# A fused two-block transformer layer: expert outputs with tokens stationary and 512 feature columns moving, and streamed activations and weight rooms on other sides of SBUF

## The chip, the core and the metric

The kernel runs as one program on one core of a Trainium2 chip. Its engines are TensorE (PE, matmuls; PEld is its loading of stationary operands), VectorE (DVE), ScalarE (ACT), GpSimd (POOL) and SyncE (SP, which issues the DMAs here). SBUF is the working memory with 128 partitions, PSUM the accumulators that PE writes. The metric is device time in microseconds, the median of several runs.

## What is computed

The reference is two blocks, one after the other, on 256 tokens of 1024 features. What matters here is the end of the first block, a mixture of 128 x 128 = 16384 experts of which each token uses 128 (8 heads, 16 each):

```python
    expert = (i1 * N_KEYS + i2).reshape(TOKEN_BLOCK, PEER_HEADS * PEER_TOPK)
    gate = jax.nn.softmax(best_s, axis=-1).reshape(TOKEN_BLOCK, PEER_HEADS * PEER_TOPK).astype(hx.dtype)
    u_sel = u[expert]
    v_sel = v[expert]
    act = jax.nn.gelu(jnp.einsum('nd,ned->ne', hx, u_sel), approximate=False)
    return jnp.einsum('ne,ned->nd', gate * act, v_sel)
```

Its result is scaled by `gate2` and added to x. The second block then projects `rms_norm_2(x) @ w_in`, runs a recurrence and a sparse attention, mixes them through `w_out`, and ends with a feed-forward part (`w_up`, a short convolution, a gelu, `w_down`).

## The kernel before

Instead of gathering experts, the kernel computes all 16384 activations for all tokens (the u loop, `u_unit`), multiplies them by a dense matrix of gates that is zero for experts not chosen (`gate_batch`), and multiplies the product by all of v (the v loop, L841 to L872).

**Weights.** All large weights come as units of 512 KB, [128, 8, 128] in fp32, in one fixed order (`stream`, L106): w1, wup1, wout1, wpq, u (128 units), v (128), w2, wup2, wout2, wff (48), wdn (24). SP loads a unit into `raw`, ACT writes its rounded part wh (L164), and DVE, or POOL for part of u, the rest wl (L165). A product is thus three matmuls: wh with the activation's high part, wh with its low part, wl with its high part (`mm3`, L188). All are of type float32r.

**Rooms.** wh and wl of a unit lie in a room, which holds a fixed number of units; a unit is split when its room has a place, up to four units ahead (`weights`, `prefetch`, L146 to L178). The plan (L139) says which room by position: w (two units, for all stages), a (stage one), b ("wwbb": two units of four, from unit 8 of w1 to the end of wout1), q, c ("wwcc", from the third unit of u to its 61st), d (three units, `spare`, v from unit 64), e ("wwe", from w2 to the end).

**Sides.** Pools are stacked from two ends of SBUF. Pools with no side or `side="left"` grow from the left: constants, raw, w, then what a stage opens. Pools with `side="right"` grow from the right end. Before the change, on the left: w, the room a, h2 (L644), the scratch of top-k, the gates' tiles (`pab`), the products `prh` and `prl` (pool pp, in h2's place), then hb, oh and hf (b2h, b2o) and xc. On the right: the first h, the room b below it, mix of the first block far down that stack, the activations actA and actB, room c below them, `spare` (the place of actA's first 24 rows), room e at the very end, and below it the attention's tiles and later ff (L1385).

**The u loop.** 128 units of 24 matmuls: stationary are 128 x 128 of weights, moving are 256 tokens of h2. Top-k of the scores runs beside the first half on DVE, one step per unit; gate batches for actA beside the second half.

**The v loop.** Per unit i, which holds 128 experts by 1024 features: for two units at a time ACT copies the gated activations into prh and DVE writes prl (L847, L848). Then 24 matmuls, for each of 8 feature blocks d three parts: stationary is u.h or u.l of block d, moving is pr with 256 tokens; the result lies in four banks vo, features on partitions. For i < 64 some 32 gate batches for actB are interleaved. Each has two products by gates (a2), two steps for b8, one for eqa on DVE, 16 small matmuls gt on PE, and a product into actB on DVE (L803); the last belongs to i = 57. From i = 64 on, every eighth unit computes one column of ada (8 of them) with the broadcast vector c (`cb`), which is loaded ahead of the loop.

**The end of v** (L875 to L900). For each of 8 feature chunks m: DVE forms x (L888, from vo, ada and x), ACT and DVE write hb's high and low part (L266, L267), and PE multiplies chunk m with the first three units of w2 (first3). A bank vo is complete once its last d is done, so the first chunks of x start while v still runs. The order of DVE's steps around it is fixed by manual dependencies (`chunk order`).

**Order.** The program's order is set by the loops; a scheduler places instructions of each engine by their dependencies and waits for tiles are set tile by tile.

## Time and profile before

| | |
|---|---|
| median of 3 runs | 1613.43 us |
| lowest, highest | 1612.01, 1619.1 us |
| profiled execution, its own time | 1618.32 us |
| its span | 1616.6 us |
| mean granted clock | 0.986 |
| PE, PEld, DVE, ACT, POOL busy | 97%, 93%, 78%, 51%, 13% of the span |
| HBM read | 277.92 MB, 173 GB/s over the span |

The profile is one execution of the program. Busy times of engines are unions of their instructions' times; the ends of matmuls are modelled, so that for matmuls the distance from one start to the next is the better measure. "Idle before" is time in which an engine stood still ahead of an instruction, with the one that released it. The granted clock is the share of TensorE's full clock (2.4 GHz).

### The profile page before, as it was taken

What the parts mean: (1) busy time and instruction counts of PE and PEld (TensorE: products, weight loads), DVE (VectorE), ACT (ScalarE), POOL (GpSimd) and SP (SyncE); (2) the same over time, 40 slices, a digit from 0 to 9 for tenths busy, and PEclk for the clock granted to TensorE, in tenths of its full rate; (3) what the DMA queues carried; (4) which work ended last, traced back from release to release, by engine and by line L of the source; (5) the groups of instructions that cost most, each with busy time, mean ns of one, the idle gap of its engine ahead of it and who ended that gap; (6) DMA issues with size and microseconds to landing.
All of it is one profiled execution on the core that took longest, in us unless ns stands there. A gap on an engine that the chain in (4) does not pass through costs nothing. (4 is left out here: it accounts for less than half of the span.)

```text
span 1616.6 us, 32864 instructions
## 1 busy us (share of the span) xinstructions
PE 1565.8 (97%) x13326; PEld 1509.9 (93%) x13326; DVE 1267.8 (78%) x2405; ACT 827.3 (51%) x1434; POOL 210.7 (13%) x156
## 2 busy tenths in 40 slices
PE   4999998999999999999999999998999999999999
PEld 3989998999999999999999999988977889999999
DVE  8789899984788887999856566979666666799963
ACT  3455563445444445443444444656656564576642
POOL 0100136795000000000000000035000000111100
PEclk9899999999999999999999999989999999999999
DMA  8668443555545545544566667453422224555553
GB/s 316 230 219 302 167 148 133 208 174 190 162 165 169 166 165 180 171 159 168 170 208 210 212 209 225 153 170 105 145 91 79 92 88 152 179 183 185 186 200 121
DMA packets 77927, 281.09 MB, mean 174 GB/s; under 512 B 8648, under 2 KB 9936, under 8 KB 77776
## 3 DMA queue, kind: packets, MB, share of 16 engines
q1 hardware_dynamic: 77776, 279.00, 51.6%
q8 instruction: 104, 1.70, 0.4%
q14 instruction: 47, 0.39, 0.1%
HBM read 277.92 MB, written 1.05 MB: 173 GB/s over the span
## 5 line engine op out<-in xcount | busy, mean ns | idle before, releaser
L164 ACT ACTIVATE wh<-raw 128x1024 fp32r<-128x1024 f32 x409 | 432.5, 1059 | 474.6 <-PE mm L188 244.8
L165 DVE TENSOR_TENSOR wl<-raw,wh 128x1024 fp32r<-128x1024 f32 x359 | 450.8, 1257 | 109.4 <-ACT wh L164 108.9
L852 PE MATMUL vo<-prh,spare 128*128 128x256 f32 x1024 | 181.1, 281 | 0.0
L852 PEld LDWEIGHTS vo<-prh,spare 128*128 128x128 f32 x1024 | 158.1, 190 | 0.0
L188 PE MATMUL mm<-h2h,wl 128*128 128x256 f32 x1024 | 143.6, 283 | 5.5 <-DVE wl L165 5.5
L188 PE MATMUL mm<-h2h,wh 128*128 128x256 f32 x1024 | 147.0, 286 | 0.0
L852 PE MATMUL vo<-prh,wh 128*128 128x256 f32 x512 | 146.7, 288 | 0.2 <-ACT prh L847 0.2
L188 PE MATMUL mm<-h2l,wh 128*128 128x256 f32 x1024 | 144.8, 285 | 0.0
L852 PE MATMUL vo<-prl,wh 128*128 128x256 f32 x512 | 144.5, 283 | 0.1
L254 POOL TENSOR_TENSOR r<-r,sq 128x256 f32<-128x256 f32 x18 | 14.5, 804 | 996.6 <-ACT sq L253 996.6
L852 PE MATMUL vo<-prh,wl 128*128 128x256 f32 x512 | 144.3, 283 | 0.0
L852 PE MATMUL vo<-prl,spare 128*128 128x256 f32 x512 | 143.9, 281 | 0.0
L165 POOL TENSOR_TENSOR wl<-raw,wh 128x1024 fp32r<-128x1024 f32 x50 | 134.2, 2701 | 68.6 <-ACT wh L164 41.6
L188 PEld LDWEIGHTS mm<-h2h,wl 128*128 128x128 f32 x1024 | 132.1, 192 | 5.9 <-DVE wl L165 5.9
L188 PEld LDWEIGHTS mm<-h2l,wh 128*128 128x128 f32 x1024 | 133.1, 193 | 0.0
L188 PEld LDWEIGHTS mm<-h2h,wh 128*128 128x128 f32 x1024 | 131.8, 192 | 0.2
L165 DVE TENSOR_TENSOR spare<-raw,spare 128x1024 fp32r<-128x1024 f32 x64 | 78.4, 1225 | 62.8 <-ACT spare L164 62.7
L164 ACT ACTIVATE spare<-raw 128x1024 fp32r<-128x1024 f32 x64 | 67.8, 1059 | 92.2 <-PE vo L852 89.5
L852 PEld LDWEIGHTS vo<-prl,wh 128*128 128x128 f32 x512 | 98.0, 191 | 0.2 <-DVE prl L848 0.2
L852 PEld LDWEIGHTS vo<-prh,wh 128*128 128x128 f32 x512 | 97.8, 191 | 0.3 <-ACT prh L847 0.3
L852 PEld LDWEIGHTS vo<-prh,wl 128*128 128x128 f32 x512 | 97.8, 191 | 0.2 <-DVE wl L165 0.2
L852 PEld LDWEIGHTS vo<-prl,spare 128*128 128x128 f32 x512 | 96.1, 188 | 0.0
(412 smaller groups left out, 3262.2 us busy)
## 6 DMA issues: line engine op xcount, KB each, us to landing
raw<-in_u_dram SPq DMA_DIRECT2D x128, 512.0 KB, 3.5
raw<-in_v_dram SPq DMA_DIRECT2D x128, 512.0 KB, 3.7
raw<-in_w_dram SPq DMA_DIRECT2D x86, 512.0 KB, 4.0
raw<-in_wada_dram SPq DMA_DIRECT2D x48, 512.0 KB, 5.0
raw<-in_wff_dram SPq DMA_DIRECT2D x48, 512.0 KB, 4.2
raw<-in_wup_dram SPq DMA_DIRECT2D x27, 512.0 KB, 4.1
raw<-in_wdn_dram SPq DMA_DIRECT2D x24, 512.0 KB, 3.5
raw<-in_wout_dram SPq DMA_DIRECT2D x16, 512.0 KB, 4.1
```

The lines of the kernel that those rows point to most:

```text
L164: S.activation(u.h, t, AF.Copy)
L165: (G if n in on_pool and on_pool[n](i) else V).tensor_tensor(u.l, t, u.h.bitcast(F32), OP.subtract)
L188: T.matmul(ps, (u.l if wl else u.h)[:, s], a[al][:, k], start=start and n == 0, stop=stop and n == len(seq) - 1)
L254: eng.tensor_tensor(tot, tot, sq, OP.add)
L852: mm = T.matmul(vo[d // 2][:, d % 2], (u.l if wl else u.h)[:, d], pr[al][:, i % 2], start=(i == 0 and n == 0 and d % 2 == 0), stop=(i == 1 ...
```

## The change

It adds one buffer of 16 KB per partition, `hot`, at the very right end of SBUF, and gives it in turn to room b (as `wpx`), h2, the v loop's products, hb, and mix2. The first 24 rows of actA, and with them `spare`, move to the left, as does room e; oh and hf (b2o) move to the right, next to `hot`. h, b1 and the other right-hand pools lie below `hot`.

In the v loop the products become the stationary operand, 128 tokens by 128 experts, and the weights the moving one, 4 feature blocks or 512 columns of u.h or u.l at a time. A unit is 12 matmuls: three parts, two halves of the tokens (b), two halves of the features (hf); the parts are now the outer loop. The four banks hold tokens on partitions. pr has three slots. The last two units are multiplied together, first all of hf 0, then all of hf 1. Then vo is copied into vt (ACT for b = 0, DVE for b = 1, one copy per half), and 16 transposes bring the features back onto partitions, in the same banks, ahead of the chunks of x; the first 8 stand in front of the loop over m, two more in each of its first four passes.

a2 and b8 share one tile `ab`, and c is loaded into such a slot at i = 64.

```diff
+    hot = ctx.enter_context(tc.tile_pool(name="hot", bufs=1, reuse_waits="tile", side="right"))
+
+    def hot_acts(name):
+        t = hot.tile([128, 2, 8, 256], F32R, name=name, tag="hot")
+        return t[:, 0], t[:, 1]
...
-        wpx = pool(hst, "wpx", 2, side="right")
...
-        rooms["a"], rooms["b"] = Room(6, wps), Room(2, wpx)
+        wpx = hot.tile([128, 2, 2, 8, 128], F32R, name="wpx", tag="hot")
+        rooms["a"] = Room(6, wps)
+        rooms["b"] = Room(2, pairs=[(wpx[:, n, 0], wpx[:, n, 1]) for n in range(2)])
...
-        hst = ExitStack()
-        h2p = pool(hst, "h2p", side="left")
+        pA0 = pool(lst, "pA0", side="left")
...
-        h2 = (h2p.tile([128, 8, 256], F32R, name="h2h"), h2p.tile([128, 8, 256], F32R, name="h2l"))
+        h2 = hot_acts("h2")
...
-            a2 = pab.tile([128, 8, 2, 64], F16, name="a2")
+            ab = pab.tile([128, 2, 1024], BF, name="ab")
+            a2 = ab[:, 1].bitcast(F16).rearrange("p (t s i) -> p t s i", t=8, s=2)
...
-            b8 = pab.tile([128, 8, 128], BF, name="b8")
+            b8 = ab[:, 0].rearrange("p (t i) -> p t i", t=8)
...
-                actA = [(0, pactA.tile([128, 24, 256], F32, name="actA0", tag="A0")),
+                actA = [(0, pA0.tile([128, 24, 256], F32, name="actA0", tag="A0")),
...
-        pp = pool(lst, "pp", 2, side="left")
+        pv_ = hot.tile([128, 8, 2, 256], F32R, name="pr", tag="hot")
+        prs = [(pv_[:, 2 * n], pv_[:, 2 * n + 1]) for n in range(3)]
...
-        vo = [pv.tile([128, 2, 256], F32, name=f"vo{i}") for i in range(4)]
-        cb = load_c(pp)
+
+        vo = [[pv.tile([128, 4, 128], F32, name=f"vo{b}{hf}") for hf in range(2)] for b in range(2)]
+        cb = None
         n0 = 0
+        held_v = []
+
+        def v_products(halves):
+            for u, pr, i in held_v:
+                for n, (wl, al) in enumerate(((0, 0), (0, 1), (1, 0))):
+                    for b in range(2):
+                        for hf in halves:
+                            T.matmul(vo[b][hf], pr[al][:, i % 2, b * 128:b * 128 + 128],
+                                     (u.l if wl else u.h)[:, 4 * hf:4 * hf + 4],
+                                     start=(i == 0 and n == 0), stop=(i == 127 and n == 2))
+
         for i in range(128):
             u = weights("v", i)
             if i % 2 == 0:
                 src = row(actA if i < 64 else actB, i % 64, 2)
-                pr = (pp.tile([128, 2, 256], F32R, name="prh"), pp.tile([128, 2, 256], F32R, name="prl"))
+                pr = prs[i // 2 % 3]
...
-            for d in range(8):
-                for n, (wl, al) in enumerate(((0, 0), (0, 1), (1, 0))):
-                    mm = T.matmul(vo[d // 2][:, d % 2], (u.l if wl else u.h)[:, d], pr[al][:, i % 2],
-                                  start=(i == 0 and n == 0 and d % 2 == 0),
-                                  stop=(i == 127 and n == 2), skip_group_check=True)
...
+            held_v.append((u, pr, i))
+            if i < 126:
+                v_products(range(2))
+                held_v.clear()
+            elif i == 127:
+                for hf in range(2):
+                    v_products([hf])
...
             elif i % 8 == 0:
+                cb = cb or load_c(pab, "ab")
                 ada_unit(cb, 40 + (i - 64) // 8)
             if i == 32:
 
-                spare = pactA.tile([128, 3, 2, 8, 128], F32R, name="spare", tag="A0")
+                spare = pA0.tile([128, 3, 2, 8, 128], F32R, name="spare", tag="A0")
...
-        rooms["e"] = Room(1, pool(ctx, "wpe", 1, side="right"))
+        rooms["e"] = Room(1, pool(ctx, "wpe", 1, side="left"))
...
-        hb = (b2h.tile([128, 8, 256], F32R, name="hbh", tag="hbh"),
-              b2h.tile([128, 8, 256], F32R, name="hbl", tag="hbl"))
+        hb = hot_acts("hb")
...
+        vtp = pool(vst, "vtp", side="right")
+        vtp.tile([128, 4096], F32, name="gap")
+        vt = [vtp.tile([128, 8, 128], F32, name=f"vt{b}") for b in range(2)]
+        for hf in range(2):
+            S.activation(vt[0][:, 4 * hf:4 * hf + 4], vo[0][hf], AF.Copy)
+            V.tensor_copy(vt[1][:, 4 * hf:4 * hf + 4], vo[1][hf])
+
+        def turned(m):
+
+            t = vo[m % 4 // 2][m // 4][:, 2 * (m % 2):2 * (m % 2) + 2]
+            for b in range(2):
+                T.transpose(t[:, b], vt[b][:, m], ident)
+            return t.rearrange("p b n -> p (b n)")
+
+        yo = [turned(m) for m in range(4)]
         for m in range(8):
-            xm = V.scalar_tensor_tensor(x[:, m], vo[m // 2][:, m % 2], ada[:, 40 + m:41 + m], x[:, m],
+            if m < 4:
+                yo.append(turned(4 + m))
+            xm = V.scalar_tensor_tensor(x[:, m], yo[m], ada[:, 40 + m:41 + m], x[:, m],
                                         op0=OP.mult, op1=OP.add)
...
-        b2o = pool(ctx, "b2o", side="left")
+        b2o = pool(ctx, "b2o", side="right")
...
-        mix = (b2h.tile([128, 8, 256], F32R, name="mix2h", tag="hbh"),
-               b2h.tile([128, 8, 256], F32R, name="mix2l", tag="hbl"))
+        mix = hot_acts("mix2")
```

## Rows read from the trace of the kernel before

**Rows 1.** The page, part 1: busy us, share of span, instructions.

```profile
PE 1565.8 (97%) x13326; PEld 1509.9 (93%) x13326; DVE 1267.8 (78%) x2405; ACT 827.3 (51%) x1434; POOL 210.7 (13%) x156
```

**Rows 2.** Busy by stretch: us; PE, PEld, DVE, ACT, POOL; granted clock, DMA share, GB/s.

```profile
225.00:355.00 130.00, 123.73 (x1011) 122.99 (x1010) 129.49 (x393) 57.97 (x92) 98.61 (x36) 0.97 0.47 163
...
420.00:620.60 200.60, 200.60 (x2040) 199.22 (x2039) 167.32 (x288) 85.30 (x127) 0.00 (x0) 1.00 0.50 167
621.80:802.00 180.20, 180.04 (x1834) 178.63 (x1835) 171.05 (x291) 77.51 (x90) 0.00 (x0) 1.00 0.51 168
823.60:1004.40 180.80, 180.80 (x1538) 180.80 (x1537) 107.25 (x124) 85.11 (x99) 0.00 (x0) 1.00 0.65 212
...
1016.00:1060.00 44.00, 42.90 (x347) 41.60 (x347) 42.77 (x77) 31.83 (x54) 5.74 (x5) 1.00 0.54 176
1088.00:1317.00 229.00, 221.75 (x1635) 191.06 (x1633) 155.04 (x306) 143.65 (x382) 22.15 (x23) 0.99 0.30 100
...
1407.70:1546.10 138.40, 137.96 (x1155) 137.71 (x1154) 129.73 (x215) 95.12 (x146) 17.79 (x24) 1.00 0.56 183
1546.20:1612.90 66.70, 66.70 (x578) 66.70 (x576) 31.32 (x34) 23.99 (x25) 0.74 (x1) 1.00 0.49 164
```

**Rows 3.** Timeline of PE in u, rooms w, then c: start us, us, instruction, count.

```profile
382.01 1.12 PE L188 MATMUL mm<-h2l,wh 128*128 128x256 f32 x8
382.97 1.12 PE L188 MATMUL mm<-h2h,wl 128*128 128x256 f32 x8
...
384.87 1.11 PE L188 MATMUL mm<-h2l,wh 128*128 128x256 f32 x8
385.81 1.10 PE L188 MATMUL mm<-h2h,wl 128*128 128x256 f32 x8
```

**Rows 4.** Timeline of PE in the down-projection, room w, then e.

```profile
1575.02 1.07 PE L188 MATMUL mm<-ffl,wh 128*128 128x256 f32 x8
1575.93 1.07 PE L188 MATMUL mm<-ffh,wl 128*128 128x256 f32 x8
1576.83 1.12 PE L188 MATMUL mm<-ffh,wh 128*128 128x256 f32 x8
```

**Rows 5.** Timeline of PE in the first block's output projection, room w.

```profile
181.80 1.11 PE L188 MATMUL mm<-mixh,wh 128*128 128x256 f32 x8
182.75 1.10 PE L188 MATMUL mm<-mixl,wh 128*128 128x256 f32 x8
```

**Rows 6.** Timeline of PE, a gate batch; and two groups, busy and mean ns.

```profile
703.95 0.64 PE L795 MATMUL gt<-a,b 128*128 128x64 f16 x16
...
L795 PE MATMUL gt<-a,b 128*128 128x64 f16 x1024 | 41.0, 194 | 0.0
...
L188 PE MATMUL mm<-hh,wh 128*128 128x258 f32 x64 | 12.1, 294 | 0.0
```

**Rows 7.** Timeline of DVE in the v loop, one cycle of two units.

```profile
704.63 0.69 DVE L803 SCALAR_TENSOR_TENSOR actB<-gt,actB 128x512 f32<-128x512 f32 x1 [0.54 <-PE gt L795]
...
710.94 0.69 DVE L803 SCALAR_TENSOR_TENSOR actB<-gt,actB 128x512 f32<-128x512 f32 x1 [0.54 <-PE gt L795]
```

**Rows 8.** Timeline of PE and DVE around the end of v.

```profile
1002.57 1.27 DVE L888 SCALAR_TENSOR_TENSOR x<-vo,ada,x 128x256 f32<-128x256 f32 x3 [1.83 <-PE vo L852]
...
1004.37 0.28 PE L852 MATMUL vo<-prh,spare 128*128 128x256 f32 x1
...
1006.91 0.39 PE L188 MATMUL mm<-hbl,wh 128*128 128x256 f32 x1 [1.91 <-DVE hbl L267]
...
1013.04 0.48 DVE L267 SCALAR_TENSOR_TENSOR hbl<-x,vec,hbh 128x256 fp32r<-128x256 f32 x1
```

**Rows 9.** Groups, and the timeline of PE, nearest to the new copies and transposes.

```profile
L847 ACT ACTIVATE prh<-actA 128x512 fp32r<-128x512 f32 x32 | 19.6, 616 | 0.0
...
392.46 0.49 PE L744 MATMUL pti<-ident,ii 128*128 128x128 f32 x3
```

**Rows 10.** Timeline of PE in the second block's attention.

```profile
1272.71 0.70 PE L1226 MATMUL sc<-kw,q 64*128 64x256 f32 x2
1273.34 0.23 PE L1228 MATMUL sc<-mk,identb 128*128 128x128 bf16 x1
```

More of the change, by code (lines that the diff above doesn't have):

```diff
@@ L271, in tile_kernel, with load_c @@
     ada = const.tile([128, 48], F32, name="ada")
-    def load_c(wpool_):
-        t = wpool_.tile([128, 1024], F32, name="cb", bufs=1)
+    def load_c(wpool_, tag):
+        t = wpool_.tile([128, 1024], F32, name="cb", tag=tag)
         nc.sync.dma_start(t, bass.AP(tensor=I["c"].tensor, offset=I["c"].offset,
@@ L833, in tile_kernel @@
                 n0 += 8
-        hst.close()
         upst.close()
-        pp = pool(lst, "pp", 2, side="left")
+        pv_ = hot.tile([128, 8, 2, 256], F32R, name="pr", tag="hot")
+        prs = [(pv_[:, 2 * n], pv_[:, 2 * n + 1]) for n in range(3)]
         vst = ExitStack()
         pv = pool(vst, "pv", side="right", space=PSUM)
-        vo = [pv.tile([128, 2, 256], F32, name=f"vo{i}") for i in range(4)]
-        cb = load_c(pp)
+        vo = [[pv.tile([128, 4, 128], F32, name=f"vo{b}{hf}") for hf in range(2)] for b in range(2)]
+        cb = None
         n0 = 0
+        held_v = []
[7 more added lines that the diff above has]
+                                     start=(i == 0 and n == 0), stop=(i == 127 and n == 2))
         for i in range(128):
@@ L845, in tile_kernel @@
                 src = row(actA if i < 64 else actB, i % 64, 2)
-                pr = (pp.tile([128, 2, 256], F32R, name="prh"), pp.tile([128, 2, 256], F32R, name="prl"))
+                pr = prs[i // 2 % 3]
                 S.activation(pr[0], src, AF.Copy)
                 V.tensor_tensor(pr[1], src, pr[0].bitcast(F32), OP.subtract)
-            first = None
-            for d in range(8):
-                for n, (wl, al) in enumerate(((0, 0), (0, 1), (1, 0))):
-                    mm = T.matmul(vo[d // 2][:, d % 2], (u.l if wl else u.h)[:, d], pr[al][:, i % 2],
-                                  start=(i == 0 and n == 0 and d % 2 == 0),
-                                  stop=(i == 127 and n == 2), skip_group_check=True)
-                    if i == 0 and n == 0:
-                        if d % 2 == 0:
-                            first = mm
-                        else:
-                            tc.add_manual_dep(mm.ins, first.ins.name, no_sync(), reason="bank start")
+            held_v.append((u, pr, i))
[5 more added lines that the diff above has]
+                    v_products([hf])
             if i < 64:
```

## The prediction

> **What bounds the kernel now.** I read the page first, for the engines' shares [rows 1]: PE is busy 97% of the span, DVE 78%. Shares are averages, so next a table by stage [rows 2], in the order of the program: top-k beside the first half of the u loop, the second half of the u loop, the v loop while gate batches run, the v loop from its second half, the two stretches of the second block's projections, the up-projection, the down-projection. What the reader is to see: PE fills every one of them but the first (123.7 of 130.0 us) and the sixth and seventh; DVE is the tight one beside top-k (129.5 of 130.0), in the gated part of the v loop (171.1 of 180.2), in the sixth (42.8 of 44.0) and in the up-projection (129.7 of 138.4). So a faster PE is worth its whole gain in the second half of v, in u and in the down-projection, and only up to DVE's floor elsewhere.
>
> Third, how far apart equal matmuls start, from the timeline (start to start of a run of 8). All are 256 columns wide. In u, 8 take 0.96 us where room w holds the weights and 0.94 where c does [rows 3]: 120 and 117.6 ns each. In the down-projection two units of three take 0.905 per 8, 113 ns, and the third, at 1.12 for the same 8, again 120 [rows 4]. In the first block's output projection the run at 181.80 takes 0.95, some 118 [rows 5]. The code says what distinguishes them. Pools grow from the left or from the right end of SBUF; w lies on the left, b, c, e and `spare` on the right. Same side for streamed tile and weights (h2 and w; ff and e): 120. Opposite sides: 117.6 to 118 (h2 left, c right; mix right, w left). Opposite with the streamed tile at the far right end and the weights left (ff and w): 113. In the v loop the same holds: 1538 matmuls in 180.8 us with `spare`, 117.6 each [rows 2], and 120 with w.
>
> **Part one: 512 columns.** In v the roles are swapped. A unit was 24 matmuls of 256 columns; it becomes 12 of 512. At 2.4 GHz (granted clock 1.00 in both v rows) 256 columns last 106.7 ns, so a 256-column matmul pays 6.3 to 13.3 ns on top. Whether 512 columns pay that once or twice the trace doesn't show: no single-pass matmul of this type is wider than 258 columns, and those stand among others [rows 6]. Bounds: the smallest extra in any dense run is the gate batch's, 16 matmuls of 64 columns in 0.64 us, the last of which alone has 194 ns, hence 29.7 each against 26.7 [rows 6], which would give 216; the largest is the extra paid per column, twice 117.6, 235. I take it once, at the spacing of opposite sides, since pr now lies right and all rooms of v left: 213.3 + 10.9 = 224 ns.
>
> The Trainium skill, "TensorE: Matmul & The Clock Gate", section "Back-to-back issue gap", gives N/2.4 + 2.5 ns for a warm matmul. The gate batch agrees (29.2 against 29.7), the 256-column rows do not (109.2 against 113 to 120). By that rule 512 columns take 215.8, and the second half of v would gain 14.9 us.
>
> Second half of v: 64 units x 12 x (235.2 - 224) = 8.6 us, bounds 0 and 14.7. DVE (107 of 181 us) and ACT (85) leave room, and PE waits for nothing there.
>
> Gated part: PE saves 58 units x 12 x (240 - 224) = 11.1 us of 180.2. But DVE does two units and a batch in 6.31 us with 0.54 of waiting, for gt [rows 7], and its busy sum is 171.1: a floor, as none of its work there is removed. I allow 2 us of waits that stay: 173, gain 7; the six units behind add 1.1. Together 8, bounds 3 and 11.
>
> Edits that I cost at nothing: pr has three slots instead of two; a2 and b8 share one slot of the same lifetime; the wl half of a unit is wanted after 8 of 12 matmuls instead of 2 of 24, which loosens the two-room chain; units 126 and 127 are multiplied together, half by half, 126 first, with three rooms to hold them. The load of c moves from before the v loop to its 65th unit on SP's queue. Its slot is free by then (the batches end by the 58th); behind it wait SP's next weight loads and, on DVE, the product for ada and then splits. DVE's 73 idle us in that half cover it; uncovered it would be some 5 us once. The single far buffer is also reused in turn: h2 behind the b room, pr behind the last u matmul, hb behind the last v matmul. In each case the writer already waits for the same moment, since pp lay where h2 was, and x needs vo.
>
> **The end of v** gets longer. Now the 8 chunks of x start before v ends: DVE's first three at 1002.57, v's last matmul at 1004.37, and PE idles 1.91 us for hbl [rows 8]. After: four copies of 128x512 out of PSUM, two on ACT (616 ns for that shape, [rows 9]) and two on DVE (0.69 us, [rows 7]), and 16 transposes at some 109 ns [rows 9]: x3 last 0.49 with 272 for one. The first half's copies lie beside the last 12 matmuls of v. On the path: the second half's copy, 0.7, then x. DVE's chain of 10.9 us (1002.57 to 1013.52) thus starts 1.0 behind the last matmul instead of 1.8 ahead, while what in it is not x's (a split of wl, 1.2) may move elsewhere: I take 2 us, between 0 and 4.
>
> **Part two: the sides.** h2, hb and mix2 go to the far right end, oh and hf next to them, room e to the left, `spare` left. So w and e with far streams should go to 113.
> - u, second half: 64 units on w x 24 x (120 - 113) = 10.8, less what is under 120 already: 9. First half: w and c alternate, DVE is full to 355 us, and c now shares its side with h2 (117.6 to 120): 31 x 24 x 7 - 30 x 24 x 2.4 = 3.5 at full gain, I take 2. Together 11, bounds 5 and 13.
> - hb: 1031 matmuls in a stretch where PE's loads cover 191 of 229 us: at most 1031 x (2/3 x 7 + 1/3 x 4.6) = 6.4, a third of the units being e's; I take 3.5. The earlier stretch is DVE's: 0.
> - oh, mix2 (384): 2.
> - hf: 1152 x (2/3 x 7 + 1/3 x 4.6) = 7.2, but DVE's floor is 129.7 of 138.4: 4.5, bounds 1 and 7.
> - ff: the e third, 192 x 7 = 1.3.
>
> **Sum:** 11 + 8 + 8.6 - 2 + 3.5 + 2 + 4.5 + 1.3 = 37. The profiled execution took 1618.3 us (span 1616.6), 4.9 above the median of the runs; 1618.3 - 37 = 1581.3, so 1576 beside the median of 1613.4.
>
> **Rivals.**
> 1. 512 columns pay almost nothing on top (216): second half of v 14.7, the gated part stops at DVE's floor: 8 us more, 1568. For it: the gate batch. Against: every 256-column row.
> 2. They pay per column (235): v gives 4 of 16.6: 1589. For it: the extra differs by side, as reading would.
> 3. 113 belongs to the down-projection, where DVE and ACT are half idle, and elsewhere opposite sides give 117.6: w gains 2.4 instead of 7; the sides give 9 of 22: 1589.
> 4. Two and three together, with the longer end: 1603 to 1613, no change that can be measured.
> 5. The weight load is no longer hidden behind its matmul. Rows that look like it: a pair of passes from kw takes 0.63 us, 315 ns each, before the next row starts [rows 10]. At 315 a unit of v takes 3.78 us instead of 2.82 to 2.88: 119 us more, less 22 for the sides, 1710. It decides from about 240 ns per matmul on, where v stops paying. Against it: 256 columns follow each other at 113 to 120, with a new load each. The Trainium skill, "TensorE: Matmul & The Clock Gate", section "The mechanism", says that loads overlap running matmuls only where the row group differs; these matmuls all use the whole array, and their spacing contradicts it.
> 6. The spacing does not depend on sides at all but on rooms' sizes or neighbours: then the change moves tiles and not times. The three spacings of one code line speak against it; it falls in with case 4.
>
> **How the numbers follow.** Forecast 0.50, rival 1 0.15, 2 0.12, 3 0.10, 4 and 6 0.07, 5 0.06. About 0.5% (8 us) is what a measurement of this kernel can tell from no change: faster means below 1605.4, slower above 1621.5. So faster 0.87, same 0.07, slower 0.06. The range takes rivals 1 to 3 and the bounds of the terms: all high gives 37 + 18 = 55, 1558; all low some 8, 1605; I cut both slightly, 1560 to 1602.
>
> **What would show it.** v's matmuls at 224 ns in the second half, and that half at 172 us; DVE at 97% or more in the gated part, at 173; u's second half near 191 us with 113 on w; hf at 134 with DVE near 97%; e's third of ff like the others; PE's gap behind v 3 to 4 us. Wrong if 512 columns lie outside 216 to 235, if u on w stays at 117 or more, or if the end of v costs over 4.

## The result, and the profile after

The changed kernel takes 1602.86 us (median of 6 runs, 1599.03 to 1604.34), the kernel before 1614.01 on the same chip: a ratio of 0.9925, 95% interval 0.991 to 0.9941. That is 11 us less, where 37 were forecast, and above the range of 1560 to 1602. The direction was right, the size was not.

The page after, part 1, answers to [rows 1]:

```profile
PE 1545.8 (97%) x11806; PEld 1414.8 (88%) x11806; DVE 1270.8 (79%) x2407; ACT 822.9 (51%) x1436; POOL 211.1 (13%) x156
```

PE has 1520 instructions less and is still busy 97% of a shorter span. The windows by stage (us; PE, PEld, DVE, ACT, POOL; granted clock, DMA share, GB/s) are, in this order: second half of u, v's first and second half, up-projection, down-projection.

```profile
415.00:614.10 199.10, 199.10 (x2052) 197.66 (x2051) 167.58 (x288) 85.33 (x129) 0.00 (x0) 1.00 0.54 170
615.40:811.70 196.30, 196.30 (x1255) 155.93 (x1256) 185.05 (x305) 88.75 (x103) 0.00 (x0) 1.00 0.56 176
811.70:990.60 178.90, 178.90 (x768) 144.16 (x767) 107.18 (x120) 84.11 (x95) 0.00 (x0) 1.00 0.70 221
1390.70:1522.40 131.70, 131.23 (x1154) 130.97 (x1154) 128.36 (x206) 87.49 (x140) 16.98 (x23) 1.00 0.59 184
1522.50:1595.80 73.30, 69.57 (x578) 69.36 (x576) 36.47 (x43) 27.06 (x30) 2.29 (x2) 0.98 0.52 164
```

Against [rows 2]: v's second half has 768 matmuls in 178.9 us, 233 ns each; 224 was forecast. The up-projection lost 6.6 us as hoped, and the down-projection took 6.7 more.

For a comparison of the main kernels below (e1 to e13 are the experiments), the stages are cut at the starts of the same matmuls in every trace. Each column is one profiled execution, in us; "end of v" is from v's last matmul to the first on hb, and "to mix2" from the last on hb to the first on mix2:

| stage | before | after | e1 | e2 | e10 | e12 | e13 |
|---|---|---|---|---|---|---|---|
| start of u | 224.3 | 221.0 | 218.2 | 224.4 | 218.3 | 217.5 | 219.1 |
| u, first half | 194.5 | 194.3 | 193.3 | 193.5 | 194.2 | 189.5 | 190.8 |
| u, second half | 203.0 | 200.1 | 203.0 | 200.1 | 193.8 | 193.8 | 193.8 |
| v, first half | 201.7 | 196.3 | 192.8 | 199.3 | 192.8 | 195.3 | 192.8 |
| v, second half | 180.8 | 179.0 | 175.6 | 180.8 | 173.9 | 180.8 | 173.9 |
| end of v | 0.1 | 2.1 | 3.2 | 0.9 | 2.1 | 0.1 | 2.1 |
| hb | 312.6 | 308.9 | 310.8 | 310.1 | 309.1 | 314.6 | 308.3 |
| to mix2 | 67.5 | 66.2 | 66.3 | 66.2 | 65.1 | 64.0 | 64.0 |
| mix2 | 23.1 | 22.8 | 23.0 | 22.8 | 22.1 | 22.1 | 22.1 |
| hf | 138.5 | 131.9 | 138.5 | 136.8 | 131.8 | 131.8 | 131.8 |
| ff | 66.6 | 73.3 | 66.6 | 67.7 | 72.3 | 73.3 | 68.4 |

The start of u lies anywhere from 216.5 to 224.4 in kernels that are the changed one up to there: 3 us there say nothing about the change. From u on the columns before and after differ by 13.5 us, the medians of the runs by 11.

**Two spacings at one place.** The timeline of PE in u after the change, all on w and h2, up to and behind the first gate batch:

```profile
409.87 1.98 PE L196 MATMUL mm<-h,wh 128*128 128x256 f32 x16
411.69 1.07 PE L196 MATMUL mm<-h,wl 128*128 128x256 f32 x8
412.59 1.98 PE L196 MATMUL mm<-h,wh 128*128 128x256 f32 x16
...
418.04 0.64 PE L804 MATMUL gt<-ab 128*128 128x64 f16 x16
418.51 2.13 PE L196 MATMUL mm<-h,wh 128*128 128x256 f32 x16
420.48 1.10 PE L196 MATMUL mm<-h,wl 128*128 128x256 f32 x8
```

Ahead of the batch 16 matmuls take 1.82 us (411.69 - 409.87), 113.7 ns each; behind it 1.97, 123 with the first one's delay, and 118 for the rest. The 113 had come in behind a unit on c and lasts until the batch; behind each later batch it is 118. The tiles are the same and lie where they lay: the sides cannot be what tells the two apart.

**The down-projection's loss.** PE's timeline there, and the clock in the stretches of the wait and behind it:

```profile
1528.18 0.99 PE L196 MATMUL mm<-ffh,wh 128*128 128x256 f32 x7
1532.90 0.39 PE L196 MATMUL mm<-ffh,wh 128*128 128x256 f32 x1 [3.73 <-ACT ffh L217]
...
1535.72 1.91 PE L196 MATMUL mm<-ffh,wh 128*128 128x256 f32 x8
1537.43 1.16 PE L196 MATMUL mm<-ffl,wh 128*128 128x256 f32 x8
```

```profile
1528.90:1532.90 4.00, 0.27 (x4) 0.07 (x2) 2.90 (x5) 1.82 (x4) 1.55 (x1) 1.00 0.64 219
1534.00:1537.40 3.40, 3.40 (x18) 3.40 (x18) 2.49 (x3) 1.06 (x1) 0.00 (x0) 0.52 0.58 195
```

PE waits 3.73 us for the last chunk of ff, then the granted clock is 0.52, the lower of its two levels (1.2 GHz), for some 3.4 us: 8 matmuls take 1.71 (1537.43 - 1535.72) instead of 0.94. And the 256-column matmuls behind it stand 118 apart, not 113 as w did in [rows 4]. The last chunk comes late for two reasons. VectorE is behind with its work for that chunk, and GpSimd's product on the way to it takes 1.55 us instead of 0.74, beside a wl step that began 0.25 earlier:

```profile
1530.60 1.22 DVE L173 TENSOR_TENSOR wl<-raw,wh 128x1024 fp32r<-128x1024 f32 x1
1530.85 1.55 POOL L1437 TENSOR_TENSOR cc<-cc,cc 128x256 f32<-128x256 f32 x1 [4.88 <-DVE cc L1433]
```

### The profile page after: what moved, and what is told of

Read it like the earlier page. It is cut to its first block, busy times and chain, and to the rows that moved or that the text cites. A ratio compares the mean times of both kernels' runs of the same rounds, so it can differ in the third digit from the quotient of the medians.

```text
span 1599.5 us, 29823 instructions
## 1 busy us (share of the span) xinstructions
PE 1545.8 (97%) x11806; PEld 1414.8 (88%) x11806; DVE 1270.8 (79%) x2407; ACT 822.9 (51%) x1436; POOL 211.1 (13%) x156
## 5 line engine op out<-in xcount | busy, mean ns | idle before, releaser
L196 PE MATMUL mm<-h,wh 128*128 128x256 f32 x2048 | 266.4, 283 | 0.0
L196 PEld LDWEIGHTS mm<-h,wh 128*128 128x128 f32 x2048 | 251.8, 191 | 0.2
L859 PE MATMUL vo<-spare,pr 128*128 128x512 f32 x768 | 179.4, 396 | 0.0
L859 PEld LDWEIGHTS vo<-spare,pr 128*128 128x128 f32 x768 | 144.4, 188 | 34.8
L196 PE MATMUL mm<-h,wl 128*128 128x256 f32 x1024 | 141.9, 281 | 8.2 <-DVE wl L173 8.2
L196 PEld LDWEIGHTS mm<-h,wl 128*128 128x128 f32 x1024 | 130.0, 190 | 8.6 <-DVE wl L173 8.6
L859 PE MATMUL vo<-wh,pr 128*128 128x512 f32 x512 | 132.5, 400 | 0.2 <-ACT pr L868 0.2
L196 PE MATMUL mm<-hb,wh 128*128 128x256 f32 x928 | 130.9, 287 | 0.3 <-ACT wh L172 0.2
L196 PEld LDWEIGHTS mm<-hb,wh 128*128 128x128 f32 x928 | 118.0, 191 | 3.1 <-ACT wh L172 1.0
L859 PEld LDWEIGHTS vo<-wh,pr 128*128 128x128 f32 x512 | 93.8, 188 | 20.3 <-ACT pr L868 0.3
```

Of the source, the lines that this page charges most:

```text
L196: T.matmul(ps, (u.l if wl else u.h)[:, s], a[al][:, k], start=start and n == 0, stop=stop and n == len(seq) - 1)
L859: T.matmul(vo[b][hf], pr[al][:, i % 2, b * 128:b * 128 + 128], (u.l if wl else u.h)[:, 4 * hf:4 * hf + 4], start=(i == 0 and n == 0), stop ...
```

## The experiments

### Each part alone

The first part alone, in the kernel before (pool pp and `spare` keep their sides):

```diff
-        vo = [pv.tile([128, 2, 256], F32, name=f"vo{i}") for i in range(4)]
+        vo = [[pv.tile([128, 4, 128], F32, name=f"vo{b}{hf}") for hf in range(2)] for b in range(2)]
...
+                            T.matmul(vo[b][hf], pr[al][:, i % 2, b * 128:b * 128 + 128],
+                                     (u.l if wl else u.h)[:, 4 * hf:4 * hf + 4],
```

> The kernel before with the first part alone: tokens stationary and 512 columns moving in v, the four copies, the 16 transposes and the joint multiplication of the last two units; every room and every streamed tile stays on its old side (the products left, spare right, w left). Theory A (the prediction: a 512-column matmul pays its extra once, opposite sides 224 ns): second half of v 172 us against 180.8, gated part 2 to 5 us less, end of v 2 longer: 1600 to 1605 us. Theory B (the extra is paid per column, 230 to 236 ns on opposite sides, 240 on the same side as w and the products are here): second half 178 to 181, gated part unchanged, end of v 2 longer: 1612 to 1616 us, no change.

Measured: 1598.98 us, ratio 0.9906 (0.9887 to 0.9924); v 192.8 and 175.6, 226 to 232 ns per matmul, end of v 3.1 longer. Neither theory: the spacing is better than in the changed kernel, although w and the products lie on one side. No difference between the first part alone and both together is shown; their intervals overlap.

The second part alone, the changed kernel with the old v loop:

> The changed kernel with the old v loop (features stationary, 256 tokens moving, no turn at its end): the second part alone. Theory A (113 ns wherever the streamed tile lies far right and the weights near the left end): v at 113, 174 us in its second half, u at 113 on w, in all some 25 us less than before, 1588. Theory B (113 is a state that PE stays in once it is in it, which it enters behind matmuls whose operands lie on one side, and leaves with any wait or gate batch; otherwise opposite sides give 117.5): v at 117.5 throughout, its second half as before, 180; u 3 us less, v's gated part 2, the first block 3, the second block 3: 1602 to 1605, nearly the whole gain of the changed kernel.

Measured: 1604.86, 0.9934 (0.9917 to 0.9952); v at 117.7 ns throughout, second half 180.8; hf at 117.8. This is theory B. Set beside e1, the turn is worth 8.9 and 5.2 us in v's halves at the old places, and only 3.0 and 1.8 at the new ones (199.3 to 196.3, 180.8 to 179.0): the second part takes from the first.

### What decides the spacing

The loops of v exchanged, so that neighbours load different stationary blocks:

```diff
-                    for b in range(2):
-                        for hf in halves:
+                    for hf in halves:
+                        for b in range(2):
```

> The changed kernel with the two inner loops of v_products exchanged, so that the tokens' half b changes from one matmul to the next and no two neighbours load the same stationary block. In the changed kernel the spacing alternates, 236 ns where the next matmul has the same stationary block and 231 where it has another. Theory A (prediction: one extra per matmul, whatever is loaded): no difference, the same alternation or none, 179 us in the second half of v. Theory B (a repeated load of the same block costs 5 ns): all at 231, second half 177, 2 to 3.5 us less in all, 1599 to 1601. Theory C (the 5 ns belong to the half of the moving unit): the alternation stays, now in pairs, time unchanged.

Measured: 1600.68, 0.9907 (0.9887 to 0.9927); 236 and 231 alternate as before, whatever is loaded, and v's second half is 179.0. This is theory A.

Room e back on the right:

```diff
-        rooms["e"] = Room(1, pool(ctx, "wpe", 1, side="left"))
+        rooms["e"] = Room(1, pool(ctx, "wpe", 1, side="right"))
```

> The changed kernel with room e put back on the right, next to the streamed tiles of the second block: a third of the units of hb, mix2, hf and ff then have both operands on one side. Theory A (address alone): e units go to 120, w units stay where they are (118 in hb, mix2 and ff, 113 in hf): 2 to 5 us slower than the changed kernel, 1605 to 1608. Theory B (state): e units at 120, and the w units behind them at 113 in mix2, hf and ff, which is 115.5 on the mean against 118 in mix2 and ff and against 113.4 in hf; DVE has more time in hf, so the 4 us of waiting and the lower clock behind it at the start of ff get shorter: ff 68 to 71 instead of 73.3, hf 133 to 135 instead of 131.7, in all 0 to 4 us less, 1599 to 1603.

Measured: 1600.69, 0.991 (0.9894 to 0.9927). PE's timeline in ff: the first rows of two units on w, the start of the unit on e that follows, and of the next on w:

```profile
1553.22 1.07 PE L196 MATMUL mm<-ffh,wh 128*128 128x256 f32 x8
1554.13 1.07 PE L196 MATMUL mm<-ffl,wh 128*128 128x256 f32 x8
...
1558.66 1.12 PE L196 MATMUL mm<-ffh,wh 128*128 128x256 f32 x8
...
1561.54 1.07 PE L196 MATMUL mm<-ffh,wh 128*128 128x256 f32 x8
```

w is at 113 behind e's 120, from the seventh unit of hf to the end of ff: theory B. Behind the very first unit on e, w still stood at 118, so one such unit does not always bring it. The kernel before shows the same at the start of ff. This is its timeline ahead of the first unit on e, the unit itself, and behind it:

```profile
1546.22 1.11 PE L188 MATMUL mm<-ffh,wh 128*128 128x256 f32 x8
1547.17 1.10 PE L188 MATMUL mm<-ffl,wh 128*128 128x256 f32 x8
...
1551.88 1.12 PE L188 MATMUL mm<-ffh,wh 128*128 128x256 f32 x8
...
1554.75 1.07 PE L188 MATMUL mm<-ffh,wh 128*128 128x256 f32 x8
1555.66 1.07 PE L188 MATMUL mm<-ffl,wh 128*128 128x256 f32 x8
```

The first unit on w takes 0.95 per 8, 118 ns, and the same room 0.91 once a unit on e has run. The 113 of [rows 4] was thus a state, a spacing that is taken at one moment and then kept, and a unit on e at 120 had brought it; the change took e to the other side, and the state went with it.

1, 2, 4 or 8 extra matmuls with both operands from h2 behind each gate batch of u:

```diff
+            for _ in range(kicks.pop() if kicks else 0):
+                T.matmul(ps, h2[0][:, 0, 0:128], h2[0][:, 0], start=True, stop=True)
```

> The changed kernel with 1, 2, 4 or 8 extra matmuls of 256 columns in turn behind the gate batches of u, ahead of the next unit, both operands from h2, hence on one side; their result is overwritten. They cost 3.75 x 0.12 us per batch, 14 us in all. Theory B (state): behind enough of them the two w units up to the next batch run at 113 instead of 117.5, 0.2 us less per batch; how many are enough shows from the four counts. Theory A (no state, a gate batch merely slows what follows in its pair of units): 117.5 behind all four counts. Time 1612 to 1617 us by A, 1606 to 1612 by B.

Measured: 1605.98 in one run, just under what theory B expected. PE's timeline in u: the rows begin behind a batch with 2 extra matmuls, then come a batch with 4 and one with 8:

```profile
443.25 2.05 PE L196 MATMUL mm<-h,wh 128*128 128x256 f32 x16
445.13 1.10 PE L196 MATMUL mm<-h,wl 128*128 128x256 f32 x8
446.07 0.64 PE L806 MATMUL gt<-ab 128*128 128x64 f16 x16
446.55 0.72 PE L776 MATMUL mm<-h 128*128 128x256 f32 x4
447.11 1.98 PE L196 MATMUL mm<-h,wh 128*128 128x256 f32 x16
448.92 1.07 PE L196 MATMUL mm<-h,wl 128*128 128x256 f32 x8
...
453.03 1.20 PE L776 MATMUL mm<-h 128*128 128x256 f32 x8
454.06 1.98 PE L196 MATMUL mm<-h,wh 128*128 128x256 f32 x16
455.88 0.39 PE L196 MATMUL mm<-h,wl 128*128 128x256 f32 x2
```

From one start to the next, 16 matmuls take 1.88 us behind 2 extra ones, 1.81 behind 4 and 1.82 behind 8. 4 and 8 bring 113 for the two units up to the next batch, 1 and 2 don't: a state, taken at an entry and kept, as theory B has it.

**The place within a line.** As built, the rooms and streamed tiles of the left stack begin at 160 beyond a multiple of 256 bytes; those of the right stack, from u on, begin at 224, and mix of the first block at 96. So "side" and "place" had been the same thing in nearly every row. Below, "distance" is the place of the moving operand minus that of the stationary one, in bytes within 256. Two kernels move the whole right stack by unused bytes, one only the products of v:

```diff
+    rpad = ctx.enter_context(tc.tile_pool(name="rpad", bufs=1, side="right"))
+    rpad.tile([128, 16], F32, name="rpad")
```

> The changed kernel with 64 unused bytes per partition at the right end of SBUF, so that everything on the right moves by 64 bytes. As built, every tile of the left stack begins at 32 and every tile of the right stack at 96 bytes beyond a multiple of 128; now both begin at 32. Theory S (sides: how far apart the two operands lie decides): nothing changes, 1600 to 1604 us. Theory P (the place within 128 bytes decides: equal places give 120 ns, unequal ones 113 or 117.5): every w unit of u, hb, mix2, hf and ff goes to 120, and c units too stay at 120; u's second half some 3.5 us longer, hf and ff together 2 to 6 us longer; v changes its pattern from 236 and 231 to that of the kernel with products on the left (226 to 232, mean 228.5), 7 us less.

> The same with 32 bytes: the right stack begins at 64 beyond a multiple of 128, the left at 32. Theory S: nothing changes, 1600 to 1604 us. Theory P: the spacings change, c units (both operands on the right, equal places) stay at 120, and w units of u (unequal by 32 bytes instead of 64) take a value that no run has shown yet, between 107 and 125 ns; 1590 to 1610 us.

> The changed kernel with the products of v alone moved by 64 bytes within their 16 KB, so that they begin at 32 beyond a multiple of 128, as the weights do. Theory S: v stays at 236 and 231, 179 us in its second half, 1600 to 1604 us. Theory P: v takes the spacing of the kernel with products on the left, 226 to 229: 174 to 176 us in the second half, 2 to 4 us less in the gated part: 1593 to 1598 us. Everything outside v stays.

Measured: e6 1604.3, 0.9939 (0.9917 to 0.9962); e7 1598.75, 0.9908 (0.9886 to 0.993); e9 1599.8, 0.9902 (0.9872 to 0.9933). Windows of e6, u's second half and v's two:

```profile
415.20:618.20 203.00, 202.78 (x2077) 201.24 (x2075) 168.94 (x289) 87.12 (x132) 0.00 (x0) 1.00 0.51 169
618.20:811.00 192.80, 192.80 (x1255) 155.66 (x1256) 183.71 (x305) 88.89 (x103) 0.00 (x0) 1.00 0.54 178
811.00:984.80 173.80, 173.80 (x768) 143.94 (x767) 107.02 (x120) 84.30 (x95) 0.00 (x0) 1.00 0.68 228
```

With equal places every 256-column matmul on w goes to 120.0, u's second half to the 203.0 of before, hf to 139.4; and 512 columns go to 226.7 ns, 173.8 for 768. The sides are those of the changed kernel, and how far apart the tiles lie is so too, but for 64 bytes. This is theory P. In e7 w is at 116.7 in hf and ff. e9 was a miss that taught something: v stayed at 232.4 (178.2 us), because 64 bytes up is equal within 128 but not within 256, where the two then lie 128 apart.

So the spacing was measured by itself, over all places:

> A kernel of float32r matmuls alone; it computes nothing of the layer and writes zeros. Stationary: 8 blocks of 128 columns, moving: 8 slices of 256, then of 512 columns, each in turn as in the layer's loops. Stationary begins at 128 beyond a multiple of 256 bytes, moving at the same place plus 0, 16, ... 240 bytes. Each distance is run twice: behind 16 matmuls of 64 columns in float16 (as behind a gate batch), and behind 16 matmuls at distance 0. Theory P (place within the line) with state: distance 0 gives 120 ns at 256 columns and 226.7 at 512; 64 (the second block's and u's case: moving 64 further) gives 117.5 behind the small matmuls and 113.3 behind distance 0, and 233.3 at 512 columns where the stationary one lies 64 further, 229 where the moving one does; the rest of the map is open, and a distance that gives 113.3 in both cases would be worth some 4.5 ns on every 256-column matmul. Theory S (sides): one spacing for all distances.

Measured (ns from start to start, worked out from the starts: the mean over the second half of each group, both groups of a distance together):

| distance | 0 | 16 | 32 | 48 | 64 | 96 | 112 | 128 | 160 | 192 | 224 |
|---|---|---|---|---|---|---|---|---|---|---|---|
| 256 columns | 120.0 | 118.7 | 117.2 | 118.4 | 117.8 | 119.9 | 113.3 | 118.6 | 118.0 | 113.3 | 118.4 |
| 512 columns | 226.7 | 231.7 | 233.3 | 233.3 | 228.9 | 233.3 | 231.1 | 233.1 | 234.4 | 233.3 | 233.3 |

The five distances that the table leaves out gave 117 to 120 and 230 to 236.7; at some distances (32 and 160 among them) the two groups differ by 1 ns or more. Four rows of PE's timeline there: a group of 40, 16 and 40 matmuls of 256 columns, the 40 at distance 192 and the 16 at 0; the same with all 96 at 0; then 24, 16 and 24 of 512 columns, in the same two ways:

```profile
272.66 11.24 PE L83 MATMUL acc<-m,w 128*128 128x256 f32 x96
284.22 11.74 PE L83 MATMUL acc<-m,w 128*128 128x256 f32 x96
590.00 15.09 PE L83 MATMUL acc<-m,w 128*128 128x512 f32 x64
605.40 14.77 PE L83 MATMUL acc<-m,w 128*128 128x512 f32 x64
```

With 256 columns the groups at 0 are the slower ones, with 512 the faster ones. Other stationary places with the same distance give the same value. Every spacing of v falls on this table, to 1 ns: 233.3 after the change (distance 192), 229 on `spare` in e1 (64) and 226.7 there on w, between the gate batches (0), 226.7 in e6 (0), 232.4 in e9 (128), 233.3 in e7 (224). This is theory P, and S falls. The twice-shown distances 64 and 192 gave one value each here, against two in the kernels; hence a second sweep:

> A kernel of float32r matmuls alone, 256 columns, that computes nothing of the layer and writes zeros. 40 matmuls at distance 64 or 192, made in two ways each (stationary at 0 and moving at 64 or 192, or the other way round), behind six kinds of matmuls: 16 small ones in float16; these and 24 at distance 0 that share the stationary, or the moving, place with the 40; the same with 25; the same with 1, 2, 4 or 8 that share the moving place; and 24 at another distance. Theory B (one of two states is taken at the entry and kept): each group of 40 runs at 113.3 or at 117.7 throughout, and what decides is whether the stationary or the moving place steps at the entry. Theory F (the state depends on the distance alone): 117.7 in all of 64 and 113.3 in all of 192, as in the sweep; then the 113.3 of w behind c in the changed kernel stays unexplained.

Measured (the last 19 of 40):

| behind | distance 64 | distance 192 |
|---|---|---|
| 16 small matmuls | 117.8 | 113.3 |
| 24 or 25 at distance 0, same stationary place | 117.8 | 113.3 |
| 24 or 25 at distance 0, same moving place | 113.3 | 117.8 |
| 1 or 2 of these | 117.8 | 113.3, once 117.7 |
| 4 or 8 of these | 113.3 | 117.7, once 113.3 |
| 24 at the other of the two distances, once each | 117.8 | 117.8 |

(In both sweeps the first groups stand without the small matmuls in front, which the scheduler placed ahead of everything.) Two rows of the timeline, each 25 matmuls at distance 0 and then 40 at 64, the first with the same stationary place and the second with the same moving place:

```profile
103.74 7.95 PE L82 MATMUL acc<-m,w 128*128 128x256 f32 x65
112.01 7.77 PE L82 MATMUL acc<-m,w 128*128 128x256 f32 x65
```

The difference, 0.18 us, is 40 times 4.5 ns. After its first ten or so, each group keeps its value: theory B. It fits w behind c, or behind e, which shares the moving place and lies at 64 (113); w behind a gate batch (118); c behind w in the kernel before, at 192 with the same moving place, 117.6 [rows 3]. Theory F falls.

What ran before does not settle it everywhere. hf in the changed kernel lies at 64; its first unit is broken by a wait and two matmuls of the norm, and the instructions there are the same as in e2, e3, e8 and e9. Behind that wait it ran at 113.3 in the changed kernel's profile and at 117.8 in those four. And u's first half in e10 and e13, which is the same code at distance 192, took 194.2 us mostly at 118 and 190.8 mostly at 113. A difference of some 5 us between single profiles can thus be the state alone.

### The places mended

> The changed kernel with its streamed tiles put at the places that the sweep found fastest: 128 unused bytes at the right end (h2, hb, mix2, oh, hf, ff then begin 64 bytes below the weights, counted within 256: distance 192, 113.3 ns in the sweep behind either kind of matmuls), the products of v 64 bytes up in their place (distance 0, 226.7 ns for 512 columns), room c 192 bytes down (it begins where w does), the y and xc tiles 192 bytes up, mix of the first block 128 down. Theory P (the place within 256 bytes decides): u's second half 193 us (200.1 in the changed kernel), v 193 and 174 (196.3 and 179.0), the second block's projections 3 to 4 us less, hf at 113 and bound by DVE, 131 to 132, ff 65 to 67: 27 to 32 us less than the changed kernel, 1571 to 1576. Theory S (sides, and state by chance): u and ff unchanged, 1598 to 1604.

```diff
+    rpad.tile([128, 32], F32, name="rpad")
...
-        pv_ = hot.tile([128, 8, 2, 256], F32R, name="pr", tag="hot")
+        pv_ = hot.tile([128, 4096], F32R, name="pr", tag="hot")[:, 16:3088].rearrange("p (a i t) -> p a i t", a=6, i=2)
...
+                pool(ust, "cpad", side="right").tile([128, 48], F32, name="cpad")
```

(and two more such pieces, for the y and xc tiles and for mix of the first block, which by the build's addresses went to distance 64 from w). Measured: 1581.47, 0.9799 (0.9776 to 0.9823). u's second half is 193.8, v 192.8 and 173.9, as theory P has it; the time is 5 above its range, since ff is 72.3 and hb gained nothing.

The kernel before with nothing but such pieces:

> The kernel before, neither part of the change, sides and loops as they were: only unused pieces of 64 or 192 bytes in front of the right end, h2, the products, hb (with oh and hf behind it), ff and mix of the first block, so that the moving tile begins 64 bytes below the stationary one (distance 192) nearly everywhere, v included, where 256 columns still move. Theory P: 113.3 in u, v, hf and ff: u's second half 193 us (203.0 before), v 192 and 174 (201.7 and 180.8), hf 131 (138.5), ff 65.5 (66.6), the rest 8 less: some 40 us less than before, 1570 to 1576, as fast as the changed kernel with its places mended. Theory S: 120 remains where tiles lie on one side, and the time is that of the kernel before, 1612 to 1618.

```diff
+    pad(ctx, 16, "right")
...
+        pad(hst, 48, "left")
         h2p = pool(hst, "h2p", side="left")
...
+        pad(lst, 48, "left")
         pp = pool(lst, "pp", 2, side="left")
```

Measured: 1593.58, 0.9856 (0.9832 to 0.988). Six pieces of 64 or 192 bytes, no loop changed, do more than the change. They miss the forecast, by some 18 us, mainly where the state went the other way: v's second half stayed at 117.8 for all 1536 matmuls and ff at 117.8, behind a wait of 3.8 us; hb took 2.0 us more. At distance 0 and 512 columns no second value has shown: that is what the turn is worth here, 180.8 against 173.9. At 113.3 throughout, the old loop would take 174.0 (an estimate, 1536 x 113.3), the same.

**What hf gives back.** In e10 too, ff takes 72.3 us and waits 3.8. One kernel gives a quarter of wff's wl steps to GpSimd:

```diff
-    on_pool = {"u": lambda i: i < 60 and (i % 4 or 22 < i < 42)}
+    on_pool = {"u": lambda i: i < 60 and (i % 4 or 22 < i < 42), "wff": lambda i: i % 4 == 1}
```

> The kernel just described with the wl half of every fourth wff unit split by GpSimd instead of VectorE (12 x 1.27 us less for VectorE; GpSimd takes 2.7 us for one). If VectorE is what holds hf at these spacings: hf 130.6 us (1152 x 113.3), no wait left at the start of ff, 1 to 3 us less than without it. If not: no difference.

Measured: 1596.24, 0.9881 (0.9854 to 0.9907), 15 us worse than e10 by the medians and 7 by the profiled executions: hf 145.2. The group of waits of PE there (us in total, times, longest):

```profile
PE mm L198 <- POOL wl L175: 8.2, 9, 1.1
```

A miss: PE waits for nine of GpSimd's twelve units. The other kernel goes the other way, and takes the product of the two branches from GpSimd to VectorE:

```diff
-            G.tensor_tensor(cv[0], cv[0], cv[1], OP.mult)
+            V.tensor_tensor(cv[0], cv[0], cv[1], OP.mult)
```

> The kernel with the places mended (e10_offsets), and in the up-projection the product of the two gelu branches taken from GpSimd to VectorE (24 steps). In the traces every second wl of hf takes 1.73 us instead of 1.22, the one beside GpSimd's product. Theory D (VectorE is what holds hf and the start of ff: its work, 5.6 us for two units against PE's 5.44, is carried over into a wait of 3.8 us in ff and a lower clock behind it): the product costs VectorE 0.42 and spares it 0.51, and the chain to the last chunk of ff is 0.3 shorter: hf and ff together 2 to 5 us less than 204.1. Theory E (the wait in ff is the chain gelu, product, split of the last chunk alone, whatever VectorE does): 0 to 0.5 us less.

Measured: 1577.63, 0.9774 (0.9755 to 0.9793); hf and ff together 200.2 instead of 204.1. VectorE's timeline at the end of hf in the changed kernel, every second wl beside GpSimd's product; then the group of wl over hf (busy us, mean ns) in e10 and in e13:

```profile
1522.93 1.22 DVE L173 TENSOR_TENSOR wl<-raw,wh 128x1024 fp32r<-128x1024 f32 x1
1524.06 1.00 DVE L1433 SCALAR_TENSOR_TENSOR cc<-zf,vec,cc 128x255 f32<-128x255 f32 x2
1524.97 0.42 DVE L1428 TENSOR_TENSOR zf<-mm,r 128x256 f32<-128x256 f32 x1
1525.31 1.75 DVE L173 TENSOR_TENSOR wl<-raw,wh 128x1024 fp32r<-128x1024 f32 x1
```

```profile
L175 DVE TENSOR_TENSOR wl<-raw,wh 128x1024 fp32r<-128x1024 f32 x46 | 66.8, 1452 | 0.0
```

```profile
L175 DVE TENSOR_TENSOR wl<-raw,wh 128x1024 fp32r<-128x1024 f32 x47 | 57.0, 1213 | 0.0
```

And the waits of PE (us in total, times, longest) that end at the last chunk of ff, in e10 and in e13:

```profile
PE mm L198 <- ACT ffh L219: 3.8, 1, 3.8
```

```profile
PE mm L198 <- ACT ffh L219: 0.6, 1, 0.6
```

This is theory D: 9.8 us less of wl against 22 products of 0.42 in that stretch, and the wait is all but gone, the lower clock with it. Two things did it. The last chunk's steps on VectorE ahead of the product begin 2.1 us sooner after the start of ff (5.0 us instead of 7.1), and from there to ffh, the chunk's rounded part, it takes 1.5 us instead of 2.7, since the product no longer stands beside a wl step. hf itself stays at 131.8, and ff ran at 118 behind the short wait, or it would have been shorter still. This is the fastest version tried, 2.3% below the kernel before, with both parts of the change in it. Whether it needs the second part is open: the turn with its places mended and the old sides was not run.

## Why the prediction was wrong, by its steps

Two terms of the sum failed, and both rest on one reading, that the sides set the spacing: 224 ns for 512 columns, and 113 on w wherever the stream lies far right. A third, hf's and ff's, took VectorE's work in one stage for that stage's alone. The outcome is nearest to rival 4, two and three together, 1603 to 1613, which had 0.07 together with rival 6; and the prediction's own sign of being wrong, u on w at 117 or more, came true.

**What bounds** was right: PE's matmuls, and their spacing. (The text counts two rows of [rows 2] one too far: the stretches that PE does not fill are the fifth and sixth, and VectorE's 42.8 of 44.0 is the fifth.)

**512 columns, "opposite sides, once": 224 ns.** Wrong, and this is the step of 8.6 + 8 us. Measured 233.3, near rival 2's price of 235. But neither "once" nor "per column" was the question: at distance 0 it is 226.7, which is twice 113.3, and the change put the products at 192. v gave 5.4 + 1.8 of 16.6 (and would have given 8.9 + 6.9, as e10 shows). Rival 1's 216 is not seen either: no run shows 512 columns below 226.7. The three spacings of 256 columns were read as a matter of sides because sides and places went together. By the places of the build the rows ahead of the prediction read: 120 at distance 0, 117.6 to 118 at 192 (c with h2, `spare` with the products, w with mix of the first block), 113 at 64 (w with ff). The change put h2, hb and hf at 64 and the products at 192.

**"113 wherever the stream is far right and the weights left".** Wrong, the step of 11 + 3.5 + 2 + 4.5 + 1.3. u's second half gave 2.9 of 9, by 118 instead of 113: rival 3 in its number (2.4 of 7 ns), rival 6 in its cause (it is not sides). u's first half gave 0.2 of 2. 113 is one of two states at distance 64, and PE is out of it after every gate batch. Places, not layout, give u its 9.2 (203.0 to 193.8). hb gave 3.7 and the stages up to mix2 1.6, near the forecast 3.5 and 2; but hb was 310.8 in e1, whose code there is that of the kernel before (312.6), so that 1.8 of the 3.7 can be chance.

**hf 4.5, ff 1.3.** Together they gave nothing: 205.1 us before, 205.2 after. hf gave 6.6 in the profiled run, where it happened to be in the state of 113 (in e2 and e3 it is at 117.8, 136.8 us); that was luck, and ff gave it back. ff took 6.7 more: 3.7 of waiting, some 1.5 of lower clock behind it (16 x 0.095), the rest by 118 throughout for 113 and 120. In e2 and e3, with hf at 118, ff does not wait, and the two take 204.5. The step that failed is "DVE's floor is 129.7 of 138.4": VectorE's work for the last chunks of ff came after the stage's last matmul, so that the floor is that of both stages together, and part of the 129.7 was time lost beside GpSimd. The Trainium skill, "SBUF — State Buffer", section "SBUF: two separate sides", says that the port pair that VectorE and GpSimd share is an exclusive lock whose loser blocks. The trace agrees both ways round: 0.52 us more for a wl (1.74 against 1.22) that begins just behind a product of 0.74, and 0.81 more for the product (1.55) that begins behind a wl. It also says that PE never waits on anyone; no run here contradicts it, for the sweep shows 113 to 120 ns by the place of PE's own two operands with no other engine at work.

**End of v, -2.** Near: the first matmul on hb comes 2.0 later behind v's last one, as forecast, but part of that is made up behind it. The end of the first three units of w2 comes 10.9 us behind v's last matmul after the change and 9.6 in e2, which has the same places and the old loop: the turn's end costs 1.3. VectorE's timeline there:

```profile
991.06 0.69 DVE L909 COPY vt<-vo 128x512 f32<-128x512 f32 x1 [2.11 <-PE vo L859]
991.67 1.26 DVE L922 SCALAR_TENSOR_TENSOR x<-vo,ada,x 128x256 f32<-128x256 f32 x3
```

The copy stands behind the last matmul, and then x, as worked out; what was 1.8 us ahead of v's last matmul in [rows 8] begins 1.0 behind it.

**Gated part.** VectorE did not stop it: it is busy 185.1 of 196.3 us, and 192.8 was reached with the same work in e1, e6 and e10. What held it was the spacing. **Loads exposed (rival 5)**: nothing of it; PEld overlaps at 226.7.

**What stays open.** Why a place costs what it does, and why at 64 and 192 two values hold, the runs don't tell. The second sweep shows which entry leads to which for matmuls alone, with two exceptions in its groups; for a stage that is entered behind a wait, as hf is, the runs show both values behind the same instructions, and not what decides. Between e1 and both parts together the runs show no difference (0.9887 to 0.9924 and 0.991 to 0.9941); which is faster is open.

## What to carry to other kernels

Before moving large tiles from one end of memory to the other, print the addresses that the build gave them, within 256 bytes, and try unused pieces of 64 bytes: here six of them were worth more than a new layout and a new loop. A spacing read from a steady stretch may be a state that an earlier stretch brought; read the start of the stage as well, and ask what in the order of units the change removes. And where a faster stage hands its work to the next, add both stages' work of the second engine before calling the gain.

## What the runs showed of the hardware

- A float32r matmul of 256 columns follows the last one after 113.3 to 120.0 ns, of 512 after 226.7 to 236.7 (granted clock 1.00, the level of 2.4 GHz), by the distance of its two operands' addresses within 256 bytes (m1, e6), and the orders differ: 0 is among the worst distances for 256 columns (96 is the other) and the best for 512.
- At distances 64 and 192 one of two values, 113.3 or 117.8, is taken at the entry and kept (m2), in one kernel for 1128 matmuls (hf after the change).
- A wl step of VectorE takes 1.74 instead of 1.22 us beside a GpSimd product of 0.74 that began before it; the product takes 1.55 where the wl step began first.
- In the changed kernel a wait of 3.7 us of PE was followed by 3.4 us at the lower level of the clock (granted 0.52).
